# Side weights of the first two k-steps: fetched and split one step at a time

## The chip, the cores and the metric

The kernel runs on one core of a Trainium2 chip. The metric is the device time of one execution in microseconds (us); runs are given by their median. The engines are named as in the profile: PE multiplies matrices (PEld is its weight load), ACT is the scalar engine, DVE the vector engine, POOL the general one, and SP only issues DMA requests. ACT can issue DMA requests as well, from the same instruction stream as its arithmetic; a q behind an engine's name (ACTq, SPq) marks an instruction of that stream which issues or waits and does no arithmetic.

## The reference, cut to what matters

One decoder block on x of shape (1, 512, 1024), in float32:

```
h    = rms_norm(x)
proj = h @ w_in                                   # GLU | q | k | v | g | gates
y_a  = silu(layer_norm(conv31(glu))) @ w_conv_proj + bias
y_b  = (silu(g) * norm(retention(rotary(q), rotary(k), v))) @ w_ret_proj
x    = x + (sigmoid(gA) * y_a + sigmoid(gB) * y_b) @ w_out
x    = x + (silu(conv3(u1)) * conv3(u2)) @ w_down     # u = rms_norm(x) @ w_up
out  = rms_norm(x)
```

Each product is computed to nearly float32 accuracy from operands that are cut in two: a rounded high part and the rest, the low part. A product is then three matmuls: high by high, high by low, low by high.

## The kernel before, in words

Everything is kept transposed: 128 channels lie on the partitions, the 512 tokens along the free dimension. All weights come as one stream `wst` of blocks of 1024 columns, in the order in which they are used. A *half* is one such block of 128x1024; it is fetched into `wraw` and cut by `cut` (L130): ACT writes the rounded high part (L131), DVE subtracts to get the low part (L132).

The beginning is different, because nothing has been fetched yet. Four output tiles are computed together by `unit_quad` (L186): for each of the eight k-steps (128 input channels each), each of the four weight tiles takes part in three matmuls, twelve per step and 96 in all, at L197. Two of the four weight tiles of a step lie side by side in one half and are called the *pair* (`load_pair`, `split_pair`; raw in `wraw`, cut into `whi` and `wlo`). The other two belong to halves 2 and 3 and are called the *side* weights: `load_side(k, n)` (L335) requests n steps from step k of each of the two, 128 columns per step, as two DMAs at L338, raw in tiles named `G`; `split_side` (L345) cuts them into tiles named `R`, with one `cut` for each of the two. The x of each step is fetched by `load_x` (L327), scaled by the column `g0` and cut by `split_scaled` (L213): ACT at L216, DVE at L217, into `xg`.

Before the change `load_side(0, 2, nc.scalar)` requests the side weights of steps 0 and 1 together, as two DMAs of 128x256 on ACT's stream. All other requests of the beginning (x, the pairs, the later side weights) go out from SP, in the order of the calls from L350 on. The split calls stand in the loop at L368: the side weights of steps 0 and 1 are cut together in the pass k = 0, behind that pass's x.

While the first data is under way, PE runs nine matmuls on a tile of ones (L318; float32 operands, so each appears as two in the trace). ACT's stream holds, before the first scaling of x, a copy of a small tile (L315), the request for `g0` (L319) and the side requests.

The order on each engine isn't quite that of the code. A planner puts every engine's instructions in order beforehand, by their priority (mostly the place in the code) and by when it reckons their operands to be there; the sums of squares at L395 are given a late priority. On the chip each stream then runs in that fixed order, and an instruction whose semaphore has not come holds up those behind it.

Of the kernel before, what the change touches and what calls it, by code (L numbers as in the profile page):

```python
# [49 lines left out]
def hybrid_block(  # L50
# [10 lines left out]
    nc = tc.nc  # L61
# [68 lines left out]
    def cut(hi, lo, raw, sl=slice(0, HS), eng=None):  # L130
        (eng or nc.scalar.copy)(out=hi[:, sl], in_=raw[:, sl])  # L131
        nc.vector.tensor_tensor(out=lo[:, sl], in0=raw[:, sl], in1=f32(hi[:, sl]),  # L132
                                op=ALU.subtract)
# [79 lines left out]
    def split_scaled(src, g, tag, bufs):  # L213
        h = t512(tag, bufs, F32R)
        l = t512(tag, bufs, F32R)
        nc.scalar.activation(out=h, in_=src, func=AF.Copy, scale=g)  # L216
        nc.vector.scalar_tensor_tensor(  # L217
            out=l, in0=src, scalar=g, in1=f32(h), op0=ALU.mult, op1=ALU.subtract)
        return h, l
# [107 lines left out]
    def load_x(k):  # L327
        nc.sync.dma_start(out=xs[k], in_=xT[k * P:(k + 1) * P, :])

    def load_pair(k, n, eng=nc.sync):  # L330
        h, c = divmod(k, 4)
        sl = slice(2 * c * P, 2 * (c + n) * P)
        eng.dma_start(out=raw01[h][:, sl], in_=wst[h][:, sl])

    def load_side(k, n, eng=nc.sync):  # L335
        h, c = divmod(k, 4)
        for i in range(2):
            eng.dma_start(out=raw23[i][h][:, c * P:(c + n) * P],  # L338
                          in_=wst[2 + i][:, k * P:(k + n) * P])

    def split_pair(k, n, eng=None):
        h, c = divmod(k, 4)
        cut(*halves[h], raw01[h], slice(2 * c * P, 2 * (c + n) * P), eng)

    def split_side(k, n):  # L345
        h, c = divmod(k, 4)
        for i in range(2):
            cut(*side[i][h], raw23[i][h], slice(c * P, (c + n) * P))

    load_x(0)  # L350
    load_pair(0, 1)
    load_side(0, 2, nc.scalar)
    load_x(1)
    load_pair(1, 1)
    load_x(2)
    load_pair(2, 2)
# [11 lines left out]
    for k in range(KT):  # L368
        if k == 0:
            split_pair(0, 1, nc.vector.tensor_copy)  # L370
        if k == 1:
            split_pair(1, 1)
        xg.append(split_scaled(xs[k], g0[:, k:k + 1], "xg", 16))
        if k == 0:
            split_side(0, 2)
        if k == 1:
            split_pair(2, 2)
            split_side(2, 2)
        if k == 3:
            split_pair(4, 2)  # L380
            split_side(4, 4)
        if k == 5:
            split_pair(6, 2)
# [101 lines left out]
    def rope(p1=None):  # L485
        p1 = p1 or unit(bank(), xg)
        p2 = unit(bank(), xg)
        res = []
        for u, v, op in ((p1, p2, ALU.subtract), (p2, p1, ALU.add)):
            m1 = tmp()  # L490
            m2 = tmp()
            nc.vector.tensor_tensor(out=m1, in0=u, in1=cosr, op=ALU.mult)
            nc.vector.tensor_tensor(out=m2, in0=v, in1=sinr, op=ALU.mult)
            nc.vector.tensor_tensor(out=m1, in0=m1, in1=m2, op=op)
            res.append(split(m1, "A", 16))
        return res
# [101 lines left out]
    for h in range(H):  # L598
# [8 lines left out]
        k = rope()  # L607
# [263 lines left out]
```

## Time and profile before

| | |
|---|---|
| median of 3 runs (lowest to highest) | 1071.82 us (1071.1 to 1072.02) |
| the profiled execution's own time | 1071.72 us |
| its span | 1069.9 us |
| PE busy | 1060.9 us, 99% of the span |
| DVE, ACT busy | 770.3 us (72%), 419.6 us (39%) |
| granted TensorE clock over the span | 0.996 of full speed |
| moved by DMA | 107.33 MB, mean 100 GB/s; 289 GB/s in the first of 40 slices |

The span reaches from the first to the last instruction of the profile; the execution's own time holds 1.8 us more. Busy times of engines overlap. A row of the timeline gives the start of a run of like instructions, its length, the engine, the line, output and inputs, their number, and in brackets how long the engine was idle before it and what ended that.

### The profile page before, as it was taken

To read this page: it belongs to the slowest core of one execution; us is meant where nothing else is said; L and a number is where in the kernel's file an instruction comes from. 1 tells how busy PE (TensorE), PEld (TensorE's weight loads), DVE (VectorE), ACT (ScalarE), POOL (GpSimd) and SP (SyncE) were. 2 spreads that over 40 slices of the span, in tenths; PEclk is the share of its full clock that TensorE was granted. 3 is DMA by queue.
4 is the path that set the end of the run, shared out by engine and by line. 5 is a ranking of instruction groups with operands and counts; after the bars stand their busy time and mean duration, and the time that the engine had idled before them with its cause. 6 is when DMAs were issued, how large, how long until landed. Compare 5 with 4: busy or idle time off the path is not lost.

```text
span 1069.9 us, 12449 instructions
## 1 busy us (share of the span) xinstructions
PE 1060.9 (99%) x4834; PEld 885.9 (83%) x4834; DVE 770.3 (72%) x1133; ACT 419.6 (39%) x561; POOL 24.4 (2%) x88
## 2 busy tenths in 40 slices
PE   9999999999999999999999999999999999999996
PEld 7888888888888888888888888888888888888886
DVE  7799899858997699957765555677776336777443
ACT  6344333533234331544552334454443113444331
POOL 0000000000000000000000000000000000000000
PEclk9999999999999999999999999999999999999998
DMA  8222232313323222223332432332222232222212
GB/s 289 91 93 102 69 99 99 108 61 103 104 89 99 70 99 99 81 78 90 108 119 97 143 119 96 106 100 99 99 99 99 99 98 93 90 96 97 99 59 79
DMA packets 34123, 107.33 MB, mean 100 GB/s; under 512 B 4048, under 2 KB 6992, under 8 KB 34064
## 3 DMA queue, kind: packets, MB, share of 16 engines
q1 hardware_dynamic: 32848, 104.42, 29.0%
q0 software_dynamic: 784, 1.85, 1.2%
q8 instruction: 38, 0.62, 0.2%
q10 hardware_dynamic: 432, 0.27, 0.1%
q14 instruction: 21, 0.17, 0.1%
HBM read 104.41 MB, written 2.11 MB: 100 GB/s over the span
## 4 chain that ended last, share of the span: by engine, by line
PE 98%; issue 1%; DVE 0%; POOL 0%; POOLq 0%; DVEq 0%
PE ps L181 27%; PE ps L180 27%; PE ps L182 27%; PE ps L507 3%; PE ps L505 3%; PE ps L506 3%; PE ps L197 2%; PE ps L563 1%; PE ps L564 1%; PE ps L562 1%; PE ps L539 0%; PE ps L541 0%; PE ps L537 0%; PE ps L318 0%; PE ps L277 0%
## 5 line engine op out<-in xcount | busy, mean ns | idle before, releaser
L131 ACT CAST whi<-wraw 128x1024 fp32r<-128x1024 f32 (+2 forms) x184 | 191.4, 1040 | 318.4 <-PE ps L181 208.3
L132 DVE TENSOR_TENSOR wlo<-wraw,whi 128x1024 fp32r<-128x1024 f32 (+2 forms) x185 | 222.6, 1203 | 59.2 <-ACT whi L131 58.0
L180 PE MATMUL ps<-xg,whi 128*128 128x512 f32 x656 | 255.6, 390 | 0.0
L181 PE MATMUL ps<-xg,whi 128*128 128x512 f32 x656 | 255.2, 389 | 0.0
L182 PE MATMUL ps<-xg,wlo 128*128 128x512 f32 x656 | 255.2, 389 | 0.0
L180 PE MATMUL ps<-A,whi 128*128 128x512 f32 x448 | 174.3, 389 | 0.0
L182 PE MATMUL ps<-A,wlo 128*128 128x512 f32 x448 | 174.3, 389 | 0.0
L447 DVE SCALAR_TENSOR_TENSOR C<-ap,par,C 128x512 f32<-128x512 f32 x240 | 166.5, 744 | 2.8 <-ACT C L444 2.6
L181 PE MATMUL ps<-A,whi 128*128 128x512 f32 x384 | 149.4, 389 | 0.0
L182 PEld LDWEIGHTS ps<-xg,wlo 128*128 128x128 f32 x656 | 123.1, 188 | 25.5
L180 PEld LDWEIGHTS ps<-xg,whi 128*128 128x128 f32 x656 | 123.2, 188 | 25.4
L181 PEld LDWEIGHTS ps<-xg,whi 128*128 128x128 f32 x656 | 123.2, 188 | 25.2
L180 PEld LDWEIGHTS ps<-A,whi 128*128 128x128 f32 x448 | 84.1, 188 | 17.6
L182 PEld LDWEIGHTS ps<-A,wlo 128*128 128x128 f32 x448 | 84.1, 188 | 17.3
L181 PEld LDWEIGHTS ps<-A,whi 128*128 128x128 f32 x384 | 72.1, 188 | 14.9
L668 DVE SCALAR_TENSOR_TENSOR t<-ap,par,t 128x512 f32<-128x512 f32 x96 | 71.7, 749 | 2.3 <-ACT t L665 0.7
L222 DVE TENSOR_TENSOR x<-x,ps 128x512 f32<-128x512 f32 (+1 forms) x50 | 32.9, 662 | 52.3 <-PE ps L182 48.8
L417 DVE TENSOR_TENSOR t<-ps,rB 128x512 f32<-128x512 f32 x48 | 32.5, 687 | 49.1 <-PE ps L182 49.1
L662 DVE TENSOR_TENSOR ap<-ps,rB 128x512 f32<-128x512 f32 x48 | 32.9, 687 | 43.5 <-PE ps L182 40.4
L180 PE MATMUL ps<-R,whi 128*128 128x512 f32 x160 | 62.2, 389 | 0.0
L181 PE MATMUL ps<-R,whi 128*128 128x512 f32 x160 | 62.2, 389 | 0.0
L182 PE MATMUL ps<-R,wlo 128*128 128x512 f32 x160 | 62.2, 389 | 0.0
(150 smaller groups left out, 1206.0 us busy)
## 6 DMA issues: line engine op xcount, KB each, us to landing
wraw<-in_wst_dram SPq DMA_DIRECT2D x180, 512.0 KB, 3.3
x<-in_xT_dram SPq DMA_DIRECT2D x16, 256.0 KB, 2.8
out_dram<-t SPq DMA_DIRECT2D x8, 256.0 KB, 2.6
nB<-row POOLq DMA_DIRECT2D x5, 256.0 KB, 4.5
dec<-in_decay_dram SPq DMA_DIRECT2D x4, 256.0 KB, 2.6
wraw<-in_wst_dram SPq DMA_DIRECT2D x3, 256.0 KB, 5.0
G<-in_wst_dram SPq DMA_DIRECT2D x2, 256.0 KB, 5.3
t<-in_cs_dram SPq DMA_DIRECT2D x2, 256.0 KB, 4.1
```

The lines of the kernel that those rows point to most:

```text
L131: (eng or nc.scalar.copy)(out=hi[:, sl], in_=raw[:, sl])
L132: nc.vector.tensor_tensor(out=lo[:, sl], in0=raw[:, sl], in1=f32(hi[:, sl]), op=ALU.subtract)
L180: nc.tensor.matmul(ps, lhsT=wh, rhs=xh, start=kt == 0, stop=False)
L181: nc.tensor.matmul(ps, lhsT=wh, rhs=xl, start=False, stop=False)
L182: nc.tensor.matmul(ps, lhsT=wl, rhs=xh, start=False, stop=kt == last)
L222: nc.vector.tensor_tensor(out=acc, in0=acc, in1=v, op=ALU.add)
L417: nc.vector.tensor_tensor(out=t, in0=ps, in1=rB[0], op=ALU.mult)
L447: nc.vector.scalar_tensor_tensor(out=acc, in0=a[:, k:k + S], scalar=wcol(k), in1=acc, op0=ALU.mult, op1=ALU.add)
L505: nc.tensor.matmul(banks[c], lhsT=xh[:, sl], rhs=wh, start=kt == 0, stop=False)
L506: nc.tensor.matmul(banks[c], lhsT=xl[:, sl], rhs=wh, start=False, stop=False)
L662: nc.vector.tensor_tensor(out=u[:, FK - 1:], in0=ps, in1=rB[0], op=ALU.mult)
L668: nc.vector.scalar_tensor_tensor(out=c, in0=u[:, k:k + S], scalar=wcol(k), in1=c, op0=ALU.mult, op1=ALU.add)
```

## The change

The requests and the cuts of the side weights of steps 0 and 1, which went together, go step by step. There are then four requests of 128x128 instead of two of 128x256, all still on ACT's stream; those of step 1 stand behind the request of x for step 1 in the code. The cuts become four on each of ACT and DVE, of 128x128 instead of two of 128x256. Step 0's cut stands in the pass k = 1, ahead of the pair and the x of that pass, step 1's behind that x.

```diff
     load_x(0)
     load_pair(0, 1)
-    load_side(0, 2, nc.scalar)
+    load_side(0, 1, nc.scalar)
     load_x(1)
+    load_side(1, 1, nc.scalar)
     load_pair(1, 1)
     load_x(2)
     load_pair(2, 2)
@@
         if k == 0:
             split_pair(0, 1, nc.vector.tensor_copy)
         if k == 1:
+            split_side(0, 1)
             split_pair(1, 1)
         xg.append(split_scaled(xs[k], g0[:, k:k + 1], "xg", 16))
-        if k == 0:
-            split_side(0, 2)
         if k == 1:
+            split_side(1, 1)
             split_pair(2, 2)
             split_side(2, 2)
```

## Rows read from the trace of the kernel before

**Rows 1.** The page, busy times: engine, us, share of the span, instructions.
```profile
PE 1060.9 (99%) x4834; PEld 885.9 (83%) x4834; DVE 770.3 (72%) x1133; ACT 419.6 (39%) x561; POOL 24.4 (2%) x88
```
**Rows 2.** Stretches: length, busy us (starts) of PE, PEld, DVE, ACT, POOL, clock, DMA.
```profile
4.85:7.58 2.73, 2.71 (x8) 1.65 (x7) 1.08 (x3) 1.40 (x4) 0.00 (x0) 1.00 0.97 326
7.58:10.37 2.79, 2.79 (x12) 2.02 (x13) 2.79 (x7) 2.79 (x7) 0.00 (x0) 1.00 1.00 312
...
28.89:50.58 21.69, 21.69 (x97) 17.99 (x96) 17.20 (x26) 8.00 (x10) 0.61 (x1) 1.00 0.28 85
```
**Rows 3.** Timeline of PE, 0 to 13 us.
```profile
0.99 4.21 PE L318 MATMUL ps<-ones 128*128 128x128 f32 x18 [0.99 <-POOL neghalf L314]
4.85 2.05 PE L197 MATMUL ps<-xg,whi 128*128 128x512 f32 x4
6.71 0.85 PE L197 MATMUL ps<-xg,wlo 128*128 128x512 f32 x2
7.58 0.73 PE L197 MATMUL ps<-xg,R 128*128 128x512 f32 x2
...
10.37 0.39 PE L197 MATMUL ps<-xg,whi 128*128 128x512 f32 x1
...
12.41 0.61 PE L197 MATMUL ps<-xg,R 128*128 128x512 f32 x2
```
**Rows 4.** Timeline of PE's weight loads, 7 to 9 us.
```profile
7.58 0.30 PEld L197 LDWEIGHTS ps<-xg,R 128*128 128x128 f32 x2 [0.54 <-ACT R L131]
...
8.40 0.19 PEld L197 LDWEIGHTS ps<-xg,R 128*128 128x128 f32 x1 [0.30 <-DVE R L132]
```
**Rows 5.** Timeline of ACT, 0 to 8 us.
```profile
0.73 0.41 ACTq L319 DMA_DIRECT2D g<-in_params_dram  x1
...
1.24 0.87 ACTq L338 DMA_DIRECT2D G<-in_wst_dram  x2
...
3.94 0.72 ACT L216 ACTIVATE xg<-x,g 128x512 fp32r<-128x512 f32 x1 [1.27 <-DMA g<-in_params_dram]
...
6.51 0.72 ACT L216 ACTIVATE xg<-x,g 128x512 fp32r<-128x512 f32 x1 [1.33 <-DMA x<-in_xT_dram]
7.14 0.39 ACT L131 CAST R<-G 128x256 fp32r<-128x256 f32 x1
```
**Rows 6.** Timeline of SP's requests, 0 to 11 us.
```profile
0.74 0.39 SPq L328 DMA_DIRECT2D x<-in_xT_dram  x1
1.18 0.42 SPq L333 DMA_DIRECT2D wraw<-in_wst_dram  x1
...
2.60 0.43 SPq L328 DMA_DIRECT2D x<-in_xT_dram  x1
3.93 0.33 SPq L333 DMA_DIRECT2D wraw<-in_wst_dram  x1
...
10.20 0.56 SPq L328 DMA_DIRECT2D x<-in_xT_dram  x1
10.80 0.43 SPq L384 DMA_DIRECT2D ident<-in_ident_dram  x1
```
**Rows 7.** Waits of SP: who waited for whom, us, times, longest.
```profile
SPq L333 <- DMA g<-in_params_dram: 0.9, 1, 0.9
```
**Rows 8.** Timeline of DVE, 0 to 11 us.
```profile
4.20 0.29 DVE L131 CAST whi<-wraw 128x256 fp32r<-128x256 f32 x1 [4.20 <-DMA wraw<-in_wst_dram]
...
10.21 0.76 DVE L132 TENSOR_TENSOR R<-G,R 128x256 fp32r<-128x256 f32 x2
```
**Rows 9.** Groups by line and form, 0 to 12 us: busy us, mean ns, idle before.
```profile
L131 ACT CAST R<-G 128x256 fp32r<-128x256 f32 x4 | 1.5, 396 | 0.0
L132 DVE TENSOR_TENSOR R<-G,R 128x256 fp32r<-128x256 f32 x4 | 1.6, 418 | 0.0
```
**Rows 10.** Line L328, the requests of x: issue to landing.
```profile
DMA to landing us min/median/max: 3.0/5.0/6.1
```
**Rows 11.** DMA issues by line, 0 to 13 us: count, KB each, us to landing.
```profile
ident<-in_ident_dram SPq DMA_DIRECT2D x1, 64.0 KB, 5.7
```

## The prediction

> **What bounds the kernel now.** I read the busy times first: PE is busy for 99% of the span, DVE for 72%, ACT for 39% [rows 1]. So a gain must come from stretches in which PE isn't at its pace, and I looked for those with the stretches [rows 2]. From 28.89 to 50.58 us there are 96 weight loads in 21.69 us, a matmul each 0.226 us. That is 512 columns at the higher clock level (2.4 GHz) and a little over. In the beginning PE is slower in two ways. The six matmuls from 4.85 to 7.58 [rows 3] are some 0.427 us apart (the row at 6.71: two in 0.85 us), which is the lower level, 1.2 GHz, although the granted clock is printed as 1.00 there [rows 2]. PE had been at it since 0.99 us with the matmuls on ones. From 7.58 us on the pace is that of the higher level. And there are small waits. Six times 0.427 is 2.56 us, and the stretch took 2.73: 0.17 lost. From 7.58 to 10.37 us eleven matmuls start (the first of them two R, the last before the row at 10.37); at 0.227 they need 2.50 us, and the stretch is 2.79: 0.29 lost. Two weight loads say what the 0.29 us is: they waited for ACT's cast of R until 7.58 and for DVE's low part of R until 8.40 [rows 4]. R are the side weights. After 10.37 us I found PE at its pace through the rest of this beginning.
>
> So all that better timed side weights can give back is 0.46 us, and the six slow matmuls, 6 x 0.20 = 1.2 us, would be touched only if the clock rose earlier. Both together are 1.7 us of 1071.72, 0.15%. What a measurement of this kernel can tell from no change is about 0.2%, 2.1 us: faster by that much is practically out. The other direction has no such lid.
>
> **Why the side weights were late.** The ACT stream [rows 5] shows it: after the first scaling and a square, ACT stood idle for 1.33 us until x of step 1 landed at 6.5 us, scaled it, and only then cast R at 7.14. The planner had put the cast behind x of step 1.
>
> **The cuts.** Two casts of 128x256 at 0.396 us and two subtractions at 0.418 [rows 9] become four of each, at half the columns. A half-size one costs at least half and at most the whole of its row: the four take between 0 and 0.8 us more on each engine. I take 0.3. It lies in ACT's 1.33 us of idle time and in DVE's wait beside it, so it costs PE nothing; if that cover were gone, it would come out of the distance that step 2 has: its last R is cut at 10.97 [rows 8] and PE comes to step 2's R at 12.41 [rows 3].
>
> With step 0's side weights cut before x of step 1, the two waits of [rows 4] go. I take 0.25 us of gain, from 0 to 0.46. What is late next is the pair of step 1, cast after that same x.
>
> **The requests.** This is the part that can hurt, because they stand on ACT's own stream. One request takes 0.43 us of its sequencer (two in 0.87, [rows 5]), so two more end at about 2.1 + 0.9 = 3.0 us if nothing holds them, before the first scaling at 3.94: free. But something holds requests. SP's sixth request, the pair of steps 2 and 3, went out at 3.93 and not at 3.03 when the fifth was done [rows 6], and it waited for the landing of `g0` [rows 7], a transfer that has nothing to do with it. By then eight requests were out: `g0` and the two side ones from ACT, five from SP. So a ninth seems to wait until the first of the eight has landed and lent it its semaphore. With four side requests, that limit comes earlier. Ordered by the rhythm of the two issuers, the eight are `g0`, x0, pair 0, x1, the two of step 0, pair 1, x2; then come the two of step 1 on ACT and SP's next between them. The first side request of step 1 then waits for `g0` (landed at about 3.93, [rows 5, 7]), the second for pair 0 (4.20, [rows 8]). The first goes out from 3.93 to 4.36, the second to 4.79. The scaling of x0 stands behind them in ACT's stream, was free at 3.94, and now starts at 4.79. Behind it wait DVE's low part of x0, and PE: the first real matmul, at 4.85 before, comes 0.85 us later, at 5.70. The matmuls on ones end at 5.20, so PE stands for half a microsecond.
>
> What that is worth on PE: if the clock rises after the same number of matmuls, the whole 0.85 us; if it rises at the same time as before, only 0.85 x 0.227/0.427 = 0.45, because the matmuls that are pushed over that point run at the higher pace. I take 0.60. On SP, the requests behind go out up to two microseconds later (the side ones of step 2 would wait for x1, at 6.5, instead of 4.3); step 2's R has 12.41 - 10.97 = 1.4 us of distance, and its cuts need not slip by all of the delay, since the requests ahead of them are the same bytes. I count nothing, at most 0.6 us.
>
> One rule of the Trainium skill speaks against the change: DMA: Bandwidth & Descriptors, Rules for kernel authors, says that many small transfers are to be joined into a large one, since under 64 KB one pays mostly overhead; 64 KB is the size of each new request. By its table of measured transfers, 0.95 us for 64 KB, the four would take 3.8 us as an estimate, and the sum would be about 1 us worse, the distance of step 2 being used up. The trace does not bear it out: `ident`, of the same 64 KB and 128x128 form, was issued at 10.80 and landed 5.7 us later [rows 6, 11], at 16.5; x7, issued at 10.20, landed at most 6.1 us later [rows 6, 10], at 16.3. So 64 KB took about 0.2 us of a full queue.
>
> **Sum.** 0.60 for the held scaling less 0.25 for the waits is +0.35 us on the profiled 1071.72 us: 1072.1. The median of the runs is 1071.82, so 0.1 above the profiled time; I leave that in the rounding.
>
> **Rivals.** First, ACT isn't held: the requests of step 1 stand behind the scaling of x0 in ACT's stream, or find semaphores free. Then only the gain is left, 0.3 us (0 to 0.46): 1071.4. For it: the planner might place late requests late. Against: at their place in the code nothing hinders them, and before, both went out long before the scaling [rows 5].
>
> Second, held and the clock as well: PE's pause puts the rise off. Before, PE had run from 0.99 to 7.56 at the lower level, 6.6 us. If after the pause it needs that again from 5.70, 12.3 us, then 15 matmuls run slow and not six, 9 x 0.20 = 1.8 us more: with 0.85 - 0.25 that is 1074.1 at the far end; in the middle between that and the forecast, 1073.1. For it: the pause falls before the rise. Against: it is short, and PE was busy on both sides. TensorE: Matmul & The Clock Gate of the Trainium skill, What's actually happening, says that the number of slow matmuls varies from run to run of one kernel, and names 6, 11 and 14; the trace has 6. By 14 the sum would be 8 x 0.20 = 1.6 us higher, before or after alike.
>
> Third, slower: the second side request of step 1 gets the semaphore of x1 instead of pair 0's. It decides on one place in the order: if SP's next two requests come in front of it, it is the twelfth request, and the fourth was x1. x1 landed at 6.50 [rows 5]; the request is out at 6.93, the scaling of x0 starts there, 3.0 us late, and so does PE's first real matmul, at 7.85. At the lower pace all of it counts, at the higher 0.53 of it: 1.6 to 3.0 us, and the pause of 2.6 us makes the upper end the nearer one. 2.8 less 0.25: 1074.3, slower by 0.23%.
>
> **Chances.** The forecast, 1072.1 (its own range 1071.6 to 1072.7): 0.45. Not held: 0.25. Clock put off: 0.16, a third of it beyond 0.2%. Held by x1: 0.10. The rest 0.04, for an order of the planner that I don't foresee, half of it slower. Faster 0.02, same 0.81, slower 0.17 (0.10 + 0.05 + 0.02). The range from 1071.0 to 1073.8 takes the forecast, most of the first rival and most of the second.
>
> **What would show it.** In the profile after: ACT's second pair of requests near 3.9 to 4.8 us with a wait for `g0` and a pair or x0, and the scaling of x0 behind them at about 4.8 instead of 3.94; PE's first real matmul near 5.7; R cast before x of step 1, with no weight load waiting on it; from 11 us on PE at 0.227 us as before. The forecast is wrong if the scaling still starts at 3.94 (first rival), if more than eight matmuls run at 0.427 (second), if a side request waits for x1 (third), or if PE waits anywhere behind 11 us.

## The result, and the profile after

The changed kernel takes 1078.13 us (median of 5 runs, 1076.5 to 1079.55), the kernel before beside it 1071.65: 1.0061 times, interval 1.005 to 1.0072. It is slower by 6.5 us, outside the range that was given (1071.0 to 1073.8). The profiled execution took 1078.66 us, 6.94 more than the one of before. The page's busy times barely differ from [rows 1], so the time is in waits:

```profile
PE 1062.4 (99%) x4834; PEld 886.8 (82%) x4834; DVE 771.5 (72%) x1135; ACT 421.1 (39%) x563; POOL 25.4 (2%) x88
```

The requests and the scaling behind them went as forecast, to the tenth; the cuts did not quite. ACT's timeline of the changed kernel:

```profile
1.24 0.88 ACTq L338 DMA_DIRECT2D G<-in_wst_dram  x2
...
3.76 1.02 ACTq L338 DMA_DIRECT2D G<-in_wst_dram  x2
4.83 0.72 ACT L216 ACTIVATE xg<-x,g 128x512 fp32r<-128x512 f32 x1 [2.17 <-DMA wraw<-in_wst_dram]
5.46 0.28 ACT L131 CAST R<-G 128x128 fp32r<-128x128 f32 x1
...
7.16 0.72 ACT L216 ACTIVATE xg<-x,g 128x512 fp32r<-128x512 f32 x1
7.78 0.28 ACT L131 CAST R<-G 128x128 fp32r<-128x128 f32 x1
...
10.51 0.62 ACT L396 ACTIVATE ss<-x 128x512 f32<-128x512 f32 x1
...
18.93 2.18 ACT L396 ACTIVATE t<-x 128x512 f32<-128x512 f32 x4
```

The second pair of side requests went out at 3.76 and ended at 4.78; the scaling of x0 behind it started at 4.83 instead of 3.94 [rows 5], and what it waited for is printed as the landing of a pair (`wraw`). Of step 0's two side weights the first is cast at 5.46, ahead of x1, as the change says. The second is cast only at 7.78, behind the scaling of x1 at 7.16: its data landed at 6.64, later than x1 (6.45). Then read on to L396, the squares of x, whose sum becomes the first RMS statistic: the first is at 10.51 us, and the last four stand together at 18.93. They had not been in the forecast's sum at all. Before, the same squares were:

```profile
4.57 0.61 ACT L395 ACTIVATE ss<-x 128x512 f32<-128x512 f32 x1
...
17.43 1.14 ACT L395 ACTIVATE t<-x 128x512 f32<-128x512 f32 x2
```

PE's timeline of the changed kernel, at four places:

```profile
5.61 1.22 PE L197 MATMUL ps<-xg,whi 128*128 128x512 f32 x2 [0.41 <-ACT xg L216]
6.62 0.50 PE L197 MATMUL ps<-xg,R 128*128 128x512 f32 x1
...
8.12 0.73 PE L197 MATMUL ps<-xg,R 128*128 128x512 f32 x2 [0.29 <-ACT R L131]
...
24.55 0.39 PE L197 MATMUL ps<-xg,R 128*128 128x512 f32 x1
26.47 0.47 PE L277 MATMUL ps<-t,onesr 128*128 128x512 f32 x1 [1.53 <-ACT t L271]
...
118.30 0.39 PE L182 MATMUL ps<-xg,wlo 128*128 128x512 f32 x1
121.31 0.50 PE L277 MATMUL ps<-t,onesr 128*128 128x512 f32 x1 [2.62 <-ACT t L271]
122.04 0.50 PE L277 MATMUL ps<-t,onesr 128*128 128x512 f32 x1 [0.22 <-DVE t L272]
...
123.24 0.63 PE L180 MATMUL ps<-xg,whi 128*128 128x512 f32 x1
```

The first real matmul is at 5.61 (4.85 in [rows 3]). At 8.12 PE waits for that second cast of R, 0.69 us behind the start of the matmul before it. By the 93rd instruction of PE the changed kernel is only 0.22 us behind. Then come two waits, both at L277, the line that sums a statistic over the partitions: 1.77 us are lost near 25 us, where the first RMS statistic isn't ready, and 3.4 us near 120, where the retention statistic of the first head isn't. (The row near 120 names ACT, L271, which rounds the finished sum; ACT itself had waited 6.5 us for DVE's last addition, L222.) Behind the second wait the clock has fallen. The stretches of the changed kernel (columns as in [rows 2]; the clock is the third number from the end):

```profile
118.69:122.86 4.17, 1.32 (x5) 0.86 (x6) 4.09 (x7) 1.57 (x2) 0.12 (x1) 1.00 0.34 126
122.86:126.50 3.64, 3.64 (x11) 2.86 (x9) 3.15 (x12) 2.38 (x3) 0.33 (x1) 0.53 0.26 65
126.50:140.00 13.50, 13.50 (x61) 11.19 (x60) 11.04 (x16) 4.95 (x8) 1.86 (x3) 1.00 0.31 89
```

PE had been busy for 1.32 of 4.17 us; then the granted clock is 0.53, about the lower level, for 3.64 us, and the matmuls there are 0.43 us apart: 1.6 us more. From 126.5 on it is back. 0.22 + 1.77 + 3.4 + 1.6 = 7.0 us, and the distance of the two kernels on PE is 6.96 from then on. After 126.5 us nothing more is lost: it stays the same up to PE's last two instructions, where 0.2 comes back.

Why the two waits hang together shows on DVE. The kernel before, then the changed one (`cosr<-t,rB` is the first use of the row of 1/rms):

```profile
19.89 1.41 DVE L222 TENSOR_TENSOR ss<-ss,t 128x512 f32<-128x512 f32 x2
21.22 1.22 DVE L132 TENSOR_TENSOR wlo<-wraw,whi 128x1024 fp32r<-128x1024 f32 x1
22.35 0.68 DVE L272 TENSOR_TENSOR t<-ss,t 128x512 fp32r<-128x512 f32 x1
...
34.67 0.69 DVE L413 TENSOR_TENSOR cosr<-t,rB 128x512 f32<-128x512 f32 x1 [4.45 <-DMA rB<-row]
...
115.18 0.76 DVE L447 SCALAR_TENSOR_TENSOR C<-ap,par,C 128x512 f32<-128x512 f32 x1
115.97 0.69 DVE L272 TENSOR_TENSOR t<-ss,t 128x512 fp32r<-128x512 f32 x1
116.58 0.68 DVE L417 TENSOR_TENSOR t<-ps,rB 128x512 f32<-128x512 f32 x1
117.18 1.22 DVE L132 TENSOR_TENSOR wlo<-wraw,whi 128x1024 fp32r<-128x1024 f32 x1
118.32 0.68 DVE L222 TENSOR_TENSOR ss<-ss,C 128x512 f32<-128x512 f32 x1
```

```profile
19.73 3.07 DVE L222 TENSOR_TENSOR ss<-ss,t 128x512 f32<-128x512 f32 x4
22.72 2.35 DVE L132 TENSOR_TENSOR wlo<-wraw,whi 128x1024 fp32r<-128x1024 f32 x2
24.99 0.68 DVE L222 TENSOR_TENSOR ss<-ss,t 128x512 f32<-128x512 f32 x1
26.36 0.69 DVE L272 TENSOR_TENSOR t<-ss,t 128x512 fp32r<-128x512 f32 x1 [0.69 <-ACT t L271]
...
38.28 0.69 DVE L414 TENSOR_TENSOR cosr<-t,rB 128x512 f32<-128x512 f32 x1 [5.11 <-DMA rB<-row]
...
118.13 0.74 DVE L448 SCALAR_TENSOR_TENSOR C<-ap,par,C 128x512 f32<-128x512 f32 x1
118.80 1.21 DVE L132 TENSOR_TENSOR wlo<-wraw,whi 128x1024 fp32r<-128x1024 f32 x1
119.93 0.68 DVE L222 TENSOR_TENSOR ss<-ss,t 128x512 f32<-128x512 f32 x1
120.53 0.68 DVE L222 TENSOR_TENSOR ss<-ss,C 128x512 f32<-128x512 f32 x1
121.29 0.69 DVE L272 TENSOR_TENSOR t<-ss,t 128x512 fp32r<-128x512 f32 x1
```

In the changed kernel the last of the eight squares is added at 24.99, behind the low parts of two halves (2.35 us) that the planner has put in front; before, the last two were added from 19.89 on. So the statistic is late (L272 at 26.36 instead of 22.35), and rB is used at 38.28 instead of 34.67, 3.6 us late. The stretches of the changed kernel show no idle time of DVE from 40 to 116 us (DVE is the third pair of numbers):

```profile
40.00:100.00 60.00, 60.00 (x274) 50.11 (x273) 60.00 (x93) 25.41 (x39) 0.00 (x0) 1.00 0.28 93
100.00:110.00 10.00, 10.00 (x60) 9.10 (x59) 10.00 (x16) 3.73 (x6) 0.00 (x0) 1.00 0.31 107
110.00:116.00 6.00, 6.00 (x28) 4.99 (x27) 6.00 (x11) 1.05 (x1) 0.12 (x1) 1.00 0.00 0
```

So what is late at 38 us is late at L272 near 120, and another 1.7 us come from the order: before, the low part of a half and a sum of the convolution (L222, ss<-ss,C) stood behind L272, now they stand in front of it. L272 is at 121.29 instead of 115.97, 5.3 us late. And there was hardly any room. In the kernel before, PE came to that statistic at 116.54, 0.57 us after DVE had begun on its second part (115.97):

```profile
116.54 0.68 PE L277 MATMUL ps<-t,onesr 128*128 128x512 f32 x2
```

An average of 72% for DVE [rows 1] hides a stretch of some 80 us in which it is at 100%.

### The profile page after: what moved, and what is told of

It is laid out like the page before. It is cut to its first block, busy times and chain, and to the rows that moved or that the text cites. A ratio compares the mean times of both kernels' runs of the same rounds, so it can differ in the third digit from the quotient of the medians.

```text
span 1076.9 us, 12458 instructions
## 1 busy us (share of the span) xinstructions
PE 1062.4 (99%) x4834; PEld 886.8 (82%) x4834; DVE 771.5 (72%) x1135; ACT 421.1 (39%) x563; POOL 25.4 (2%) x88
## 4 chain that ended last, share of the span: by engine, by line
PE 87%; DVE 8%; issue 2%; DMA 1%; ACT 1%; POOL 0%; SPq 0%; POOLq 0%; DVEq 0%
PE ps L181 25%; PE ps L180 25%; PE ps L182 25%; DVE C L448 3%; PE ps L508 2%; PE ps L507 2%; PE ps L506 2%; DVE wlo L132 2%; DMA x<-in_xT_dram 1%; PE ps L564 1%; PE ps L565 1%; PE ps L563 1%; DMA rB<-row 0%; DVE t L418 0%; PE ps L277 0%
## 5 line engine op out<-in xcount | busy, mean ns | idle before, releaser
L222 DVE TENSOR_TENSOR x<-x,ps 128x512 f32<-128x512 f32 (+1 forms) x50 | 32.8, 660 | 52.3 <-PE ps L182 48.8
```

Source lines behind the costliest of these rows:

```text
L222: nc.vector.tensor_tensor(out=acc, in0=acc, in1=v, op=ALU.add)
```

## The experiments

**Theory A**: the requests on ACT's stream make the planner put the squares late; rB is late; DVE carries that to the retention statistic, where PE waits. **Theory B**: the finer cuts cost the time. **Theory C**: with eight requests outstanding at most, x3 to x7 land about 1.1 us later, and that carries through whatever the order. The kernel before, run beside these, took 1071.35 us beside the first four and 1071.59 beside the last four.

**The requests alone.**

```
-    load_side(0, 2, nc.scalar)
+    load_side(0, 1, nc.scalar)
     load_x(1)
+    load_side(1, 1, nc.scalar)
```

> The requests alone go step by step on ACT's stream (as in the changed kernel); the cuts stay as before. Theory A (late statistic: the requests on ACT's stream make the planner put the squares of x late, so the row of 1/rms lands late, PE waits at the statistic's matmul near 25 us and again at the first retention statistic near 120 us): first square of x behind 9 us, rB about 3 us late, both waits there, 1076 to 1079. Theory B (the finer cuts on ACT and DVE are what costs): 1071.5 to 1072.5. Theory C (the limit of eight outstanding requests makes x3 to x7 land about 1.1 us later, and that carries through): as A in time, 1076 to 1079, with x7 landing near 17.4 us; the next kernel but one tells A from C.

1076.74 us, 1.0053 times (1.004 to 1.0066). The first square is at 11.73 and the timeline of DVE has rB late and L272 late:

```profile
37.42 0.69 DVE L414 TENSOR_TENSOR cosr<-t,rB 128x512 f32<-128x512 f32 x1 [3.39 <-DMA rB<-row]
...
120.98 0.69 DVE L272 TENSOR_TENSOR t<-ss,t 128x512 fp32r<-128x512 f32 x1 [0.68 <-ACT t L271]
```

As A and C say. One thing differs: PE lost 2.45 us already before 12 us, 1.5 of them waiting for R, since the undivided cut of steps 0 and 1 now needs the late requests too, and 0.9 in matmuls at 0.43 us behind that wait. It then came late enough to the first statistic to wait little there (0.36 us between the starts). The end is the same, set at L272: the clock didn't fall in this execution, and it is 5.02 us over the kernel before, with L272 5.01 us late.

**The cuts alone.**

```
+            split_side(0, 1)
             split_pair(1, 1)
         xg.append(split_scaled(xs[k], g0[:, k:k + 1], "xg", 16))
-        if k == 0:
-            split_side(0, 2)
         if k == 1:
+            split_side(1, 1)
```

> The cuts alone go step by step; the requests stay two of 128x256. A and C: no loss, 1071.0 to 1072.5, first square near 4.6 us, rB near 34.7. B: the loss of the changed kernel, 1076 to 1079.

1072.83 us, 1.0018 times (1.0009 to 1.0027): a small part, not nothing. The first square is at 4.26, rB at 35.70 and L272 at 118.50, 2.5 us late (1.0 of it from rB); in the profiled execution (1075.96, the slowest of eleven) PE's wait there was followed by a stretch at the lower clock level. B fails for the most part; A's bound of 1072.5 was too low, because the order near 115 us, with the low part of a half ahead of L272, came up here as well.

**Step 1's side requests on SP.**

```
-    load_side(1, 1, nc.scalar)
+    load_side(1, 1)
```

> The changed kernel, but step 1's two side requests are issued by SP, in the same place of the code; all four stay 64 KB, so as many requests are outstanding. A: ACT's stream is free again, the scaling of x0 starts near 3.9, the squares are early, no wait near 25 and 120 us: 1071.0 to 1072.5. C: x7 still lands about 1 us later than before and the loss stays: 1075 to 1079.

1072.07 us, 1.0009 times (1.0 to 1.0018). The timeline of ACT in this kernel:

```profile
3.62 0.72 ACT L216 ACTIVATE xg<-x,g 128x512 fp32r<-128x512 f32 x1 [0.95 <-DMA g<-in_params_dram]
4.25 0.61 ACT L396 ACTIVATE ss<-x 128x512 f32<-128x512 f32 x1
```

All but 0.7 us of the loss is gone, as A says. All four requests are still of 64 KB. Against C this run says less than it seems: x3 and x4 land at 10.91 and 11.55, nearly as late as in the changed kernel (11.19, 11.82; before 9.86, 10.66), but x5 to x7 land only some 0.45 us later than before, against 1.1 to 1.2 in the changed kernel. The run with the squares in another order, below, settles it. At the 93rd instruction PE is 0.75 us ahead of the kernel before, but 0.6 us of that is given back near 116 us, where it waits for the retention statistic. Part of the lead is the clock's: the matmuls reach the higher pace near 6.0 us in this execution, near 7.6 in that of before.

**The statistic late, all else as before.** Five needless multiplications by one:

```
+    for _ in range(5):
+        nc.vector.tensor_scalar(out=ss.acc, in0=ss.acc, scalar1=1.0, scalar2=None, op0=ALU.mult)
     stat(ss.acc, D, EPS, norm_mix, (1, 2), "rB")
```

> The kernel before, with five needless multiplications by one on DVE (0.4 us each) between the sum of squares and its matmul: the start, the requests and the squares stay as they were, only the statistic is late, by about 2.1 us, or 3.3 with the half that the planner lets by. A: rB 2 to 3.5 us late, a wait of PE at the statistic near 23 us (0.5 to 2 us) and one near 117 us, the sum of all waits being the delay of rB plus what a fallen clock costs: 1074 to 1078. B and C (the statistic has room): 1071.5 to 1072.5.

1078.30 us, 1.0064 times (1.0052 to 1.0077): the whole loss of the changed kernel, without any of its edits, and a little more than the 1074 to 1078 that was expected. rB is used at 38.60, 3.9 us late, where 2 to 3.5 was expected; in the profiled execution x7 landed 0.9 us later than before as well, which has nothing to do with the multiplications. PE's timeline of this kernel:

```profile
26.99 0.47 PE L277 MATMUL ps<-t,onesr 128*128 128x512 f32 x1
...
121.59 0.80 PE L277 MATMUL ps<-t,onesr 128*128 128x512 f32 x1 [3.93 <-ACT t L271]
```

The planner moved the first statistic's matmul back on PE, so there was hardly a wait near 25 us (0.4 us between the starts; a wait of 0.5 to 2 was expected); nearly all of it came at 121, 4.3 us between the starts, and ten matmuls at the lower level behind it.

**The retention statistic's matmul later on PE.**

```
-        stat(sq.acc, DV, EPS, use, (2, 2), "nB")
+        stat(sq.acc, DV, EPS, use, (3, 2) if h == 0 else (2, 2), "nB")
```

> The changed kernel, but the matmul that sums the first head's retention statistic stands one unit of 24 matmuls (5.4 us) later in PE's order. Theory A (PE waits at 118 us because DVE, busy from the landing of rB on, brings the statistic late): DVE still has it at about 121.3 us, PE comes to it at about 124, the wait of some 3.5 us there goes and with it the matmuls at the lower clock level: 1072.8 to 1074.3, that is 4 to 5 us under the changed kernel; the wait near 25 us stays. Rival (the loss near 118 us has another cause, or only moves back by one unit): 1077 to 1079.

1073.69 us, 1.0023 times (1.0014 to 1.0031). DVE begins on the statistic's second part at 119.92, PE comes to it at 123.49 and doesn't wait:

```profile
123.49 0.61 PE L277 MATMUL ps<-t,onesr 128*128 128x512 f32 x2
```

The start and the wait near 25 us (1.2 us here) stay, and so do about 2 us of the loss; 4.4 us of it are gone with one number.

**The first statistic's matmul later on PE.**

```
-QSUM = 5
+QSUM = 6
```

> The changed kernel, but the first statistic's matmul stands one k-step later in the code (five matmuls, 1.1 us, later in PE's order). Theory A (what counts is when DVE gets rB and how far that carries to the statistic near 118 us): the wait near 25 us shrinks by about 1.1 us, rB lands no earlier, and PE, being earlier at 118 us, waits that much longer there: 1077.5 to 1079, no gain. Rival (the two waits are separate losses that add up): 1.1 us of gain, 1076.5 to 1077.2.

1078.80 us, 1.0068 times (1.0055 to 1.0081): no gain. The loss near 25 us shrinks from 1.77 to some 0.7 us, and PE waits the longer at 121.54:

```profile
25.99 0.47 PE L277 MATMUL ps<-t,onesr 128*128 128x512 f32 x1
...
121.54 0.49 PE L277 MATMUL ps<-t,onesr 128*128 128x512 f32 x1 [4.01 <-ACT t L271]
```

So the gains at the two waits don't add up. The later one takes back whatever the earlier one is spared.

**The squares in another order, the requests still on ACT.** Each square behind its scaling in the code, the last two with a higher priority:

```
         xg.append(split_scaled(xs[k], g0[:, k:k + 1], "xg", 16))
+        with tc.high_priority(offset=0 if k < 6 else 200):
+            ss.add(xs[k])
...
-    with tc.high_priority(offset=-200):
-        for i in range(KT):
-            ss.add(xs[i])
```

> The changed kernel with its requests on ACT, but each square of x stands right behind its scaling in the code, the last two before that: only the planner's order of the squares and sums is another. Theory A (the held requests hurt through the order of the squares): rB lands near 35 to 37 us instead of 38.3, and the loss shrinks to 0.5 to 4 us: 1072 to 1075.5. Theory C (the late landings of x set the statistic, whatever the order): 1077 to 1079.

1073.98 us, 1.0022 times (1.0013 to 1.003). rB is at 35.34, L272 at 118.14:

```profile
35.34 0.69 DVE L413 TENSOR_TENSOR cosr<-t,rB 128x512 f32<-128x512 f32 x1 [3.16 <-DMA rB<-row]
...
118.14 0.67 DVE L272 TENSOR_TENSOR t<-ss,t 128x512 fp32r<-128x512 f32 x1
```

The requests still hold ACT (first real matmul at 5.33), and two thirds of the loss are gone by the order alone. This is what fails C: x3 to x7 land as late as in the changed kernel (x3 at 11.14, x7 at 17.55, there 11.19 and 17.44), and rB is 2.9 us earlier all the same.

**Step 1's side requests on SP, and the retention statistic later.**

```
-    load_side(1, 1, nc.scalar)
+    load_side(1, 1)
...
-        stat(sq.acc, DV, EPS, use, (2, 2), "nB")
+        stat(sq.acc, DV, EPS, use, (3, 2) if h == 0 else (2, 2), "nB")
```

> Step 1's side requests on SP, and the first head's retention statistic one unit later on PE. With SP's requests PE was 0.75 us ahead of the kernel before until 116 us and then waited 0.5 us for that statistic. Theory A: the wait goes, the lead stays: 1070.4 to 1071.2 against 1071.4, the best of all. Rival (the lead is given back elsewhere): 1071.4 to 1072.2.

1071.24 us against 1071.59, 0.9997 times (0.9988 to 1.0006): well ahead of the changed kernel, and not to be told from the kernel before, so that the expected lead is not shown. The profiled execution keeps a lead of 0.85 us to the end (span 1069.5 against 1069.9; the shorter span is less than the lead because the executions differ in the last microseconds too). A lead of that size is under what these runs can tell.

One relation runs through all profiles. L272 follows the first use of rB by 82.8 to 83.6 us in the nine kernels other than that of before (81.3 there; it alone has the low part of a half behind L272 and not in front), and where PE waits at it, the execution is late by what L272 is late plus some 0.2 us for each matmul at the lower level: 2.2 and 2.3 us for the reordered squares, 5.0 and 5.0 for the requests alone, 5.3 and 6.9 for the changed kernel with its eight slow matmuls. The farthest off is the kernel with the multiplications: 5.6 and 7.1 with ten, half a microsecond less than this relation gives. Why the planner puts the squares late when ACT issues two more requests stays open; the order is plain to see, its reckoning isn't in the profile.

## Why the prediction was wrong, point by point

- **The held requests**: right. The forecast had them from 3.93 to 4.79, behind `g0` and pair 0; they went from 3.76 to 4.78. The scaling of x0 was forecast at 4.79 and came at 4.83, the first real matmul at 5.70 and came at 5.61.
- **Their price**: right in its sum, and that in part by luck. The sum was +0.35 us; at the 60th instruction of PE the distance was 0.36. But the terms were others. The first real matmul was 0.76 us late. The 0.25 us of gain from the waits on R did not come: the second side weight of step 0 was cast behind x1 at 7.78, and PE lost 0.46 us to it at 8.12, against the sign "no weight load waiting on it". Its data landed at 6.64 (7.10 in the kernel before), later than x1; the forecast had looked at the order of the casts and not at that landing. (And of the two waits in [rows 4] the one until 7.58 belongs to the 0.17 us lost ahead of it, not to the 0.29; their total of 0.46 stands.) What made up for it, some 0.7 us, was the clock: the matmuls reached the higher pace near 6.7 us, not near 7.6. In the ten profiled executions they reach it anywhere from 4.2 to 7.6 us, and the kernel with the later first statistic, whose beginning is the same program, near 6.0. So the second rival (a later rise) didn't occur. The third (a request that waits for x1 on ACT) didn't occur; x1 held a request of SP, the side weights of step 2, until 6.47.
- **"I count nothing, at most 0.6 us" for what comes behind, and "from 11 us on PE at 0.227 us as before"**: the step that failed. Step 2 did arrive in time, but that was the wrong thing to hold the delay against. The thing that was late was the sum of squares, which stands under a late priority (`offset=-200`) and so goes where the planner finds room. The forecast had seen a square in ACT's stream and left it out of the sum. 1.77 + 3.4 + 1.6 us hung on it. Its own last sign, "if PE waits anywhere behind 11 us", is the one that came.
- **ACT's idle 1.33 us as a cover**: it was read as if the rest of ACT's stream would stay in its order, but the planner makes that order anew for each kernel. Two more requests in the stream moved the first square from 4.57 to 10.51, far more than the 0.9 us that they took.
- **The chance of 0.04 for an order of the planner that isn't foreseen** was far too small for an edit that changes what stands on ACT's stream. The other direction "has no such lid", the prediction says, and then it gives that direction no price beyond 1074.3.

The weighed rule, DMA: Bandwidth & Descriptors of the Trainium skill, Rules for kernel authors (join small transfers), would have had the four requests themselves as the cost. With step 1's side weights on SP, still four requests of 64 KB, 0.7 of the 6.5 us was left, at the edge of what these runs can tell: the measurement decides, and the size wasn't the main cost here. The 0.95 us that the prediction took from that page of the Trainium skill stands there, in the section Bandwidth, for transfers issued from GpSimd (POOL), and these were issued from ACT.

## What to carry to other kernels

Look for the result that every engine waits for, and for its room, before pricing an edit near the start: here a row of 1/rms, with an engine that is at 100% from its landing to the next statistic. A DMA request in the stream of an engine that also computes isn't a matter of its issue time alone: it can wait for the landing of an older request, and it shifts the order of all that the planner would fill in there. When two waits lie in a row behind one late result, mending the first may be worth nothing until the second is mended: here the first wait fell by 1.1 us and the time didn't.

## What the runs showed that was not expected

The clock fell after some short waits and not after others. PE idle for 2.62 and 0.22 us around 120 us was followed by eight matmuls at 0.43 us (granted clock 0.53); with idle times of 1.27 and 0.58 us in the kernel with the cuts alone also eight; with 1.64 and 0.22 us in the kernel with the requests alone none. This may be part of the spread of the runs (the cuts alone: 1072.28 to 1075.96, and its profiled execution, with the eight, was the slowest); only profiled executions show it, so it stays a guess.
